# Key and query evacuation in pairs with pinned transposes, high parts of weights on GpSimd, modulation rows moved into attention

## The chip, the cores and the metric

The kernel runs on one core of one Trainium2 chip. The metric is the time of one execution in microseconds (us), lower is better. It is taken as the median of several executions; one more execution was recorded by the hardware profiler, and every row below is from that one. Engines are called TensorE (PE in the rows; PEld is its weight load), VectorE (DVE), ScalarE (ACT), GpSimd (POOL) and SyncE (SP, which issues the DMAs).

## The reference, cut to what matters

The model has two layers over 512 latent tokens of width 1024. Layer 0 mixes by attention (12 query heads, 4 key heads, 64 wide, over 512 latent and 256 context keys) and by a Fourier transform of four groups; layer 1 is a convolution module. Each layer ends with a squared-ReLU MLP, and every sub-layer is scaled and shifted by rows computed from the conditioning vector. What the change touches is this part of layer 0:

```python
def project(h):
    p = h @ w_in
    q = rms_norm(p[..., :D_Q].reshape(bsz, l, N_Q_HEADS, HEAD_DIM), q_g)
    k = rms_norm(p[..., D_Q:D_Q + D_KV].reshape(bsz, l, N_KV_HEADS, HEAD_DIM), k_g)
    v = p[..., D_Q + D_KV:D_Q + 2 * D_KV].reshape(bsz, l, N_KV_HEADS, HEAD_DIM)
    f = p[..., D_Q + 2 * D_KV:]
    return q, k, v, f
...
qx = apply_rope(qx, cos, sin)
kx = apply_rope(kx, cos, sin)
```

The rows of modulation are `m = s @ ada_w + ada_b` with `s = silu(c)`, 6 x 1024 values per layer.

## The kernel before

Products keep the accuracy of 32-bit floats by splitting each operand into a high and a low part in a rounded format: every product is three matmuls, high by high, high by low, low by high (`products`, lines 322 to 324; `three`, lines 184 to 186). Weights come in blocks of 1 MB: SyncE loads one into a `raw` tile (two buffers), an engine writes the high part into `w` and another subtracts it from `raw` for the low part. In `Stream.split` the high part is ScalarE's (line 164); who makes the low part (line 167) says the table `EARLY`, 0 for VectorE and 1 for GpSimd: blocks 3, 4, 5 of the input projection, both Fourier blocks and the first output block were GpSimd's. Each projection or Fourier block is split in pieces of 512 or 516 columns.

The order of the program is: load, conditioning and normalization (to about 40 us of the span); keys and values; queries; attention; then the output projection, the MLPs and the convolution. Rows are handled in tiles of 128 tokens. Keys and values have six tiles (`kv`, two of context `chl` and four latent `act`), each with 24 matmuls of 512 columns in two halves with the weight blocks w0 and w1, into the six banks `kv_ps`. The inputs of the second half are made by `context(1)` and `latent(1, h)` through `affine_split`: GpSimd makes an affine row `aff` (line 220), ScalarE the high part, VectorE subtracts (line 221). Queries come in two groups `g` of four tiles: group 1 is four heads and the Fourier columns, group 2 eight heads; each tile has 24 matmuls.

`evac_kv` takes a key tile out of its bank: ScalarE copies the values and squares the keys, VectorE sums (`ss`, line 505) and makes the inverse root in `rsqrt_small` (lines 208 to 213, with a logarithm and an exponential on ScalarE between), scales (`kn`, line 515), applies gain or rotation (`kr`), and the high and low part go into a stage `st` (lines 525 to 528). Eight transposes by TensorE (line 532) and two copies (line 537) put it into `kA` and `kB`. `evac_q` does the same for queries (lines 549 to 559), with `rq` for the inverse root. The transposes' banks `tbank` have two buffers, `st` has two. The 14 evacuations of one tile each stand in the program behind the products of their stage, and a scheduler in the tile layer may move any instruction that is not pinned (`pin`, `tc.keep_in_program_order`).

The modulation rows are VectorE's: one `gemv_tile` (line 231) multiplies a 128x1024 tile of weights `gv` by a broadcast vector and accumulates into `mods`. The program has 80 of them. `gemv(n, pool, per)` loads `per` tiles by one DMA and does them. With `GV = (0, 3)` twelve stand in the evacuation of group 1's query tiles, three behind each, one tile for each DMA into the pool `gvp`, and the scheduler moves them up; with `GV_AT = (8, 10)` two loads of two tiles each follow the groups 8 and 10 of attention's units.

Attention has 48 units (`softmax`): scores (lines 446 and 448), a maximum on VectorE (line 451), the exponential on ScalarE, the division on GpSimd (line 458), a `flip` by transposes (line 634), and `weigh` on the values. Four units are a group; three units (`AHEAD`) are scored ahead of the first flip.

## Time and profile before

| what | value |
|---|---|
| median of 3 runs | 1216.81 us |
| runs, lowest and highest | 1213.05 and 1807.99 us |
| profiled execution | 1216.12 us |
| its span, first to last instruction | 1214.2 us |
| mean granted clock of TensorE | 0.989 of full |
| TensorE busy | 1175.0 us, 97% of the span |
| VectorE, ScalarE, GpSimd busy | 770.3, 510.7, 196.4 us |

The profiled execution lies between the lowest and the median run, and 1.9 us of it are outside the span. Busy shares are means over stages with different limits, so a change in one stage is read from that stage's own rows. Times in the rows are microseconds from the start of the span.

### The profile page before, as it was taken

To read this page: it belongs to the slowest core of one execution; us is meant where nothing else is said; L and a number is where in the kernel's file an instruction comes from. 1 tells how busy PE (TensorE), PEld (TensorE's weight loads), DVE (VectorE), ACT (ScalarE), POOL (GpSimd) and SP (SyncE) were. 2 spreads that over 40 slices of the span, in tenths; PEclk is the share of its full clock that TensorE was granted. 3 is DMA by queue.
4 is the path that set the end of the run, shared out by engine and by line. 5 is a ranking of instruction groups with operands and counts; after the bars stand their busy time and mean duration, and the time that the engine had idled before them with its cause. 6 is when DMAs were issued, how large, how long until landed. Compare 5 with 4: busy or idle time off the path is not lost.

```text
span 1214.2 us, 16309 instructions
## 1 busy us (share of the span) xinstructions
PE 1175.0 (97%) x6356; PEld 983.0 (81%) x6356; DVE 770.3 (63%) x1395; ACT 510.7 (42%) x931; POOL 196.4 (16%) x236
## 2 busy tenths in 40 slices
PE   5988889999999999999999999999999999999998
PEld 2666777667998888888888988889998888888887
DVE  5797767655787665576465889989953343443431
ACT  5545477774443232142232624387641231331320
POOL 3653243430000000000003037640000000000000
PEclk9998999999999999999999999999999999999999
DMA  8652114105356655544543232613332322233201
GB/s 321 255 189 76 53 35 139 36 1 209 104 174 242 213 204 208 204 176 178 205 173 104 72 113 84 226 64 139 106 104 104 104 104 90 84 104 104 101 21 52
DMA packets 26204, 160.22 MB, mean 132 GB/s; under 512 B 2704, under 2 KB 5776, under 8 KB 8464
## 3 DMA queue, kind: packets, MB, share of 16 engines
q1 hardware_dynamic: 26128, 159.19, 36.7%
q8 instruction: 50, 0.82, 0.3%
q14 instruction: 26, 0.21, 0.1%
HBM read 157.08 MB, written 2.10 MB: 131 GB/s over the span
## 4 chain that ended last, share of the span: by engine, by line
PE 88%; DVE 6%; DMA 1%; POOL 1%; issue 1%; ACT 1%; SPq 0%; DVEq 0%; ACTq 0%; POOLq 0%
PE mm L185 24%; PE mm L186 24%; PE mm L184 24%; PE po L651 3%; PE mm L879 3%; PE tp L634 3%; PE sc L446 2%; PE sc L448 1%; POOL aff L220 1%; DVE gv L231 1%; DMA gv<-in_adat 1%; DMA cx<-in_ctxT 1%; PE sc L324 1%; DVE sm L451 0%; PE tp L384 0%
## 5 line engine op out<-in xcount | busy, mean ns | idle before, releaser
L185 PE MATMUL mm<-act,w 128*128 128x512 f32 (+1 forms) x992 | 338.2, 342 | 0.6 <-DVE act L1061 0.5
L186 PE MATMUL mm<-act,w 128*128 128x512 f32 (+1 forms) x992 | 337.5, 341 | 0.0
L184 PE MATMUL mm<-act,w 128*128 128x512 f32 (+1 forms) x992 | 337.3, 342 | 0.0
L164 ACT ACTIVATE w<-raw 128x1024 fp32r<-128x1024 f32 (+2 forms) x204 | 178.7, 909 | 240.5 <-PE mm L186 202.0
L184 PE MATMUL mm<-f,w 128*128 128x512 f32 (+1 forms) x560 | 207.8, 371 | 0.0
L185 PE MATMUL mm<-f,w 128*128 128x512 f32 (+1 forms) x560 | 207.8, 371 | 0.0
L186 PE MATMUL mm<-f,w 128*128 128x512 f32 (+1 forms) x560 | 207.7, 371 | 0.0
L185 PEld LDWEIGHTS mm<-act,w 128*128 128x128 f32 x992 | 187.8, 190 | 22.6 <-DVE act L1061 1.4
L184 PEld LDWEIGHTS mm<-act,w 128*128 128x128 f32 x992 | 187.2, 190 | 22.2 <-ACT act L1071 0.7
L186 PEld LDWEIGHTS mm<-act,w 128*128 128x128 f32 x992 | 187.8, 190 | 21.4
L167 DVE TENSOR_TENSOR w<-raw,w 128x1024 fp32r<-128x1024 f32 (+1 forms) x172 | 179.8, 1074 | 26.4 <-ACT w L164 26.3
L767 DVE SCALAR_TENSOR_TENSOR x<-mm,mods,x 128x512 f32<-128x512 f32 (+1 forms) x82 | 55.8, 684 | 171.6 <-PE mm L186 171.5
L167 POOL TENSOR_TENSOR w<-raw,w 128x512 fp32r<-128x512 f32 (+2 forms) x32 | 57.9, 1829 | 460.2 <-ACT w L164 460.1
L821 DVE TENSOR_TENSOR rsq<-relu 128x512 f32<-128x512 f32 (+1 forms) x76 | 45.8, 607 | 122.7 <-ACT relu L818 122.6
L818 ACT ACTIVATE relu<-mm 128x512 f32<-128x512 f32 (+1 forms) x76 | 40.3, 530 | 195.4 <-PE mm L186 194.3
L185 PEld LDWEIGHTS mm<-f,w 128*128 128x128 f32 x560 | 105.5, 188 | 18.5 <-DVE f L822 0.3
L184 PEld LDWEIGHTS mm<-f,w 128*128 128x128 f32 x560 | 105.5, 188 | 18.2
L186 PEld LDWEIGHTS mm<-f,w 128*128 128x128 f32 x560 | 105.5, 188 | 18.0
L231 DVE SCALAR_TENSOR_TENSOR gv<-gv,sbc 128x1024 f32<-128x1024 f32 x80 | 99.4, 1256 | 9.8 <-DMA gv<-in_adat 9.8
L868 DVE SCALAR_TENSOR_TENSOR sb<-u,vecs,sb 128x512 f32<-128x512 f32 x112 | 75.3, 749 | 0.0
L451 DVE TENSOR_REDUCE sm<-sc 128x1 f32<-128x768 f32 x48 | 45.9, 955 | 25.5 <-PE sc L448 24.2
L458 POOL TENSOR_SCALAR p<-p,sm 128x768 f32<-128x768 f32 x48 | 47.1, 982 | 73.8 <-DVE sm L457 49.8
(232 smaller groups left out, 1377.7 us busy)
## 6 DMA issues: line engine op xcount, KB each, us to landing
raw<-in_w SPq DMA_DIRECT2D x64, 1024.0 KB, 4.8
gv<-in_adat SPq DMA_DIRECT2D x34, 1024.0 KB, 5.3
raw<-in_pw SPq DMA_DIRECT2D x12, 1024.0 KB, 4.9
w<-in_diag SPq DMA_DIRECT2D x8, 1152.0 KB, 5.7
ar<-in_ada SPq DMA_DIRECT2D x8, 1024.0 KB, 9.4
raw<-in_w_in SPq DMA_DIRECT2D x6, 1024.0 KB, 5.5
gv<-in_adat SPq DMA_DIRECT2D x12, 512.0 KB, 4.5
raw<-in_w_out SPq DMA_DIRECT2D x4, 1024.0 KB, 4.9
```

The costliest lines, as they stand in the source:

```text
L164: hi = nc.scalar.activation(w[:, 0, r], raw[:, r], AF.Copy)
L167: eng.tensor_tensor(w[:, 1, r], raw[:, r], w[:, 0, r].bitcast(F32), ALU.subtract)
L184: nc.tensor.matmul(ps, lhsT=whi, rhs=xhi, start=first, stop=False)
L185: nc.tensor.matmul(ps, lhsT=whi, rhs=xlo, start=False, stop=False)
L186: nc.tensor.matmul(ps, lhsT=wlo, rhs=xhi, start=False, stop=last)
L231: nc.vector.scalar_tensor_tensor(r, r, 1.0, sbc, ALU.mult, ALU.mult, accum_out=mod(l, j, t))
L451: nc.vector.tensor_reduce(sm[:, 0:1], sc[:, :NK], AX.X, ALU.max)
L458: nc.gpsimd.tensor_scalar(p, p, sm[:, 3:4], 0.0, ALU.mult, ALU.add)
L767: nc.vector.scalar_tensor_tensor(xs, ps, mod(l, j, t), xs, ALU.mult, ALU.add)
L818: nc.scalar.activation(r, ps, AF.Relu)
L821: nc.vector.tensor_tensor(s, r, r, ALU.mult)
L868: tap = nc.vector.scalar_tensor_tensor(vs if j == TAPS - 2 else a, u[:, t, j:j + S], w[j], a, ALU.mult, ALU.add)
```

## The change

- `HIGH_POOL` names blocks whose high part GpSimd makes now, by a copy with rounding (CAST in the order): the input projection's blocks 2 to 5 and both Fourier blocks. `EARLY` is gone: the low parts of all these blocks are VectorE's; the first output block's low part stays GpSimd's.
- `rsqrt_small` becomes `rsqrt_pair`: one inverse root for two tiles, and the factor that came behind it is folded into scale and addend. Fourteen become seven.
- `evac_kv` becomes `keys(n)` for a pair of key tiles, which ends at the stage `st`, and `place_key`, which does the transposes and copies later. The scaling `kn` is made by ScalarE as four copies of 64 columns with a scale for each head. `evac_q` becomes `queries` and `place_query` in the same way. `st` has four buffers, the root's tiles two.
- The products of this stage and the transposes of the placements, but those of the last two query tiles, are pinned to the order in which they are written. The second half of key tiles 2 to 5 moves behind `keys(0)`, and `QUERY_ORDER` with the list `after` says after which product slot a placement stands.
- `GV` is gone, and `GV_AT` has eight groups: 16 modulation tiles in attention, by eight loads of 1 MB, where there were four.

```diff
+HIGH_POOL = (2, 3, 4, 5, 6, 7)
...
-GV = (0, 3)
-GV_AT = (8, 10)
+GV_AT = (4, 5, 6, 7, 8, 9, 10, 11)
...
-EARLY = (0, 0, 0, 1, 1, 1, 1, 1, 1, 0, 0, 0)
+QUERY_ORDER = ((0, 0), (0, 1), (1, 0), (1, 1), (0, 2), (0, 3), (1, 2), (1, 3))
...
         def split(self, k, eng, w, raw, r):
-            hi = nc.scalar.activation(w[:, 0, r], raw[:, r], AF.Copy)
-            if k in PINNED:
-                tc.keep_in_program_order(hi)
+            if k in HIGH_POOL:
+                self.high(k, eng, w, raw, r)
+            else:
+                hi = nc.scalar.activation(w[:, 0, r], raw[:, r], AF.Copy)
+                if k in PINNED:
+                    tc.keep_in_program_order(hi)
...
-    def rsqrt_small(pool, dst, ss, n, dim, post):
-        v = pool.tile([P, 16], F32, name="rss_v", tag="rss_v")[:, :n]
-        y = pool.tile([P, 16], F32, name="rss_y", tag="rss_y")[:, :n]
-        nc.vector.tensor_scalar(v, ss, 1.0 / dim, EPS, ALU.mult, ALU.add)
+    def rsqrt_pair(pool, dst, ss, n, scale, add):
+        v = pool.tile([P, 16], F32, name="rss_v", tag="rss_v", bufs=2)[:, :2 * n]
+        y = pool.tile([P, 16], F32, name="rss_y", tag="rss_y", bufs=2)[:, :2 * n]
+        nc.vector.tensor_scalar(v, ss, scale, add, ALU.mult, ALU.add)
         nc.scalar.activation(y, v, AF.Ln)
         nc.scalar.activation(y, y, AF.Exp, scale=-0.5)
         nc.vector.tensor_tensor(v, v, y, ALU.mult)
         nc.vector.scalar_tensor_tensor(v, v, -0.5, y, ALU.mult, ALU.mult)
-        nc.vector.scalar_tensor_tensor(dst, v, 1.5, y, ALU.add, ALU.mult)
-        if post != 1.0:
-            nc.vector.tensor_scalar_mul(dst, dst, post)
+        nc.vector.scalar_tensor_tensor(dst, v.rearrange("p (a n) -> p a n", a=2), 1.5,
+                                       y.rearrange("p (a n) -> p a n", a=2), ALU.add, ALU.mult)
...
-    blocks = [(w_in[i], (vec_, pool_)[EARLY[i]], 4) for i in range(6)]
-    blocks += [(dft[i], (vec_, pool_)[EARLY[6 + i]], 2) for i in range(2)]
-    blocks += [(w_out[i], (vec_, pool_)[EARLY[8 + i]], OUT_CUT) for i in range(4)]
+    blocks = [(w_in[i], vec_, 4) for i in range(6)]
+    blocks += [(dft[i], vec_, 2) for i in range(2)]
+    blocks += [(w_out[i], (pool_, vec_)[i > 0], OUT_CUT) for i in range(4)]
...
-        def products(ps, unit, w, half):
+        def products(ps, unit, w, half, fixed=False):
...
+                for a, e, first, last in ((hi, 0, kt == 0, False), (hi, 1, False, False),
+                                          (lo, 0, False, kt == KT - 1)):
+                    i = nc.tensor.matmul(ps, lhsT=a, rhs=w[:, e, k], start=first, stop=last)
+                    if fixed:
+                        pin(i)
...
-                products(kv_ps[n_], kv[n_], w1, 1)
+                products(kv_ps[n_], kv[n_], w1, 1, True)
             for h in range(2):
                 latent(1, h)
-                for n_ in (2 + 2 * h, 3 + 2 * h):
-                    products(kv_ps[n_], kv[n_], w1, 1)
...
-            def evac_kv(ps, kt, tt):
...
-                rsqrt_small(wk, rk, ss, NKV, HD, 1.0)
-                kn = wk.tile([P, 512], F32, name="kn", tag="kn", bufs=2)[:, :256]
-                nc.vector.tensor_tensor(heads(kn, NKV), heads(kp, NKV),
-                                        rk.unsqueeze(2).to_broadcast([P, NKV, HD]), ALU.mult)
...
+            def transposed(st, step, dst, fixed):
+                pt = tbank()
+                for h in range(4):
+                    i = nc.tensor.transpose(out=pt[:, h * P:(h + 1) * P],
+                                            in_=st[:, h * step:h * step + 128], identity=ident)
+                    if fixed:
+                        pin(i)
+                nc.scalar.activation(dst, pt.rearrange("p (h t) -> p h t", h=4), AF.Copy)
+
+            stages = {}
+
+            def keys(n):
+                ss = wk.tile([P, 16], F32, name="ss", tag="ss", bufs=2)[:, :2 * NKV]
+                for i in range(2):
+                    ps = kv_ps[n + i]
+                    sumsq(ps[:, 0:256], NKV, ss[:, i * NKV:(i + 1) * NKV])
+                    nc.scalar.activation(vS[:, kv[n + i][2]], ps[:, 256:512], AF.Copy)
+                rk = wk.tile([P, 2, NKV], F32, name="rk", tag="rk", bufs=2)
+                rsqrt_pair(wk, rk, ss, NKV, 1.0 / HD, EPS)
+                for i in range(2):
+                    _, _, kt, tt = kv[n + i]
+                    kn = wk.tile([P, 512], F32, name="kn", tag="kn", bufs=2)[:, :256]
+                    for h in range(NKV):
+                        r = slice(h * HD, (h + 1) * HD)
+                        nc.scalar.activation(kn[:, r], kv_ps[n + i][:, r], AF.Copy,
+                                             scale=rk[:, i, h:h + 1])
+                    kr = wk.tile([P, 512], F32, name="kr", tag="t2", bufs=2)[:, :256]
+                    if tt is None:
+                        nc.vector.tensor_tensor(heads(kr, NKV), heads(kn, NKV),
+                                                bc_heads(gs[:, 2], NKV), ALU.mult)
+                    else:
+                        rope_apply(kr, kn, tk, tt, NKV)
+                    st = wk.tile([P, 1024], F32, name="st", tag="st", bufs=4)
+                    sk = st[:, :NKV * 192].rearrange("p (h e d) -> p h e d", h=NKV, e=3)
+                    nc.scalar.activation(sk[:, :, 0].bitcast(F32R), heads(kr, NKV), AF.Copy)
+                    nc.vector.tensor_tensor(sk[:, :, 1].bitcast(F32R), heads(kr, NKV), sk[:, :, 0],
+                                            ALU.subtract)
+                    nc.scalar.activation(sk[:, :, 2].bitcast(F32R), heads(kr, NKV), AF.Copy)
+                    stages["k", n + i] = st
+
+            def place_key(n):
+                st = stages.pop(("k", n))
+                kt = kv[n][2]
                 for e, dst in ((0, kA), (1, kB)):
+                    transposed(st[:, e * 64:], 192, dst[:, :, kt * P:(kt + 1) * P], True)
...
-            def evac_q(ps, tt, h0, n):
...
+            def queries(ps, g, t0):
+                n, h0 = ((4, 8), (8, 0))[g - 1]
+                ss = wk.tile([P, 16], F32, name="ss", tag="ss", bufs=2)[:, :2 * n]
+                for i in range(2):
+                    sumsq(ps[t0 + i][:, :n * HD], n, ss[:, i * n:(i + 1) * n])
+                rsqrt_pair(wk, rq[:, t0:t0 + 2, h0:h0 + n], ss, n, 1.0, HD * EPS)
+                for i in range(2):
+                    tt = t0 + i
+                    qr = wk.tile([P, 512], F32, name="kn", tag="kn", bufs=2)[:, :n * HD]
+                    rope_apply(qr, ps[tt][:, :n * HD], tq, tt, n)
+                    st = wk.tile([P, 1024], F32, name="st", tag="st", bufs=4)
+                    sq_ = st[:, :n * 128].rearrange("p (h e d) -> p h e d", h=n, e=2)
+                    nc.scalar.activation(sq_[:, :, 0].bitcast(F32R), heads(qr, n), AF.Copy)
+                    nc.vector.tensor_tensor(sq_[:, :, 1].bitcast(F32R), heads(qr, n), sq_[:, :, 0],
+                                            ALU.subtract)
+                    if g == 1:
+                        evac_f(ps[tt][:, 256:], tt)
+                    stages[g, tt] = st
+
+            def place_query(g, tt, fixed=True):
+                n, h0 = ((4, 8), (8, 0))[g - 1]
+                st = stages.pop((g, tt))
                 for q4 in range(n // 4):
+                    transposed(st[:, q4 * 512:], 128,
+                               qT[:, h0 + q4 * 4:h0 + q4 * 4 + 4, tt * P:(tt + 1) * P], fixed)
 
...
-            for n_, (_, _, kt, tt) in enumerate(kv):
-                evac_kv(kv_ps[n_], kt, tt)
-                if tt is not None:
-                    gemv(GV[0], gvp, 1)
+            keys(0)
+            for n_ in range(2, 6):
+                products(kv_ps[n_], kv[n_], w1, 1, True)
+                if n_ >= 4:
+                    place_key(n_ - 4)
+                if n_ % 2 == 1:
+                    keys(n_ - 1)
+            after = {1: [lambda i=i: place_key(i + 2) for i in range(4)], 2: []}
             for g in (1, 2):
                 ps = [mbank(m) for m in SLOTS[g]]
                 w = [split_k(next_w()) for _ in range(2)]
-                for half, j in [(half, j) for half in range(2) for j in range(4)] if g == 1 else \
-                        [(half, j) for j in range(4) for half in range(2)]:
-                    products(ps[j], (act, j), w[half], half)
-                for j in range(4):
-                    if g == 1:
-                        evac_q(ps[j][:, :256], j, 8, 4)
-                        evac_f(ps[j][:, 256:], j)
-                        gemv(GV[1], gvp, 1)
-                    else:
-                        evac_q(ps[j], j, 0, 8)
+                for slot, (half, j) in enumerate(QUERY_ORDER):
+                    products(ps[j], (act, j), w[half], half, True)
+                    if after[g]:
+                        after[g].pop(0)()
+                    if slot in (3, 7):
+                        queries(ps, g, slot // 2 - 1)
+                        if g == 1 or slot == 3:
+                            after[g if slot == 3 else 2] += [lambda: None] + [
+                                lambda g=g, t=t: place_query(g, t)
+                                for t in (slot // 2 - 1, slot // 2)]
+            for t in (2, 3):
+                place_query(2, t, False)
             for n_ in range(AHEAD):
                 score(n_)
 
```

The order of instructions on TensorE before, around the end of the key products and the first transposes (`sc` and `po` are the banks of products, `tp` those of transposes, `st` the stages of key tiles; `w1_142` is the second weight block, `w2_511` the third):

```order
L323 MATMUL sc_101<-w1_142,act_79 128x512
L324 MATMUL sc_101<-w1_142,act_79 128x512
L532 MATMUL tp_706<-ident_67,st_702 128x128 x4
L532 MATMUL tp_712<-ident_67,st_702 128x128 x4
L322 MATMUL sc_100<-w2_511,act_79 128x512
L323 MATMUL sc_100<-w2_511,act_79 128x512
L324 MATMUL sc_100<-w2_511,act_79 128x512
L532 MATMUL tp_740<-ident_67,st_736 128x128 x4
L532 MATMUL tp_746<-ident_67,st_736 128x128 x4
```

The order on TensorE now, from the key products of the third pair to the third placement:

```order
L326 MATMUL po_103<-w1_142,act_79 128x512 x12
L326 MATMUL sc_101<-w1_142,act_79 128x512 x12
L511 MATMUL tp_755<-ident_67,st_658 128x128 x4
L511 MATMUL tp_761<-ident_67,st_658 128x128 x4
L326 MATMUL sc_101<-w1_142,act_79 128x512 x12
L511 MATMUL tp_779<-ident_67,st_669 128x128 x4
L511 MATMUL tp_785<-ident_67,st_669 128x128 x4
L326 MATMUL sc_100<-w2_511,act_79 128x512 x12
L511 MATMUL tp_871<-ident_67,st_725 128x128 x4
L511 MATMUL tp_877<-ident_67,st_725 128x128 x4
```

The first two placements stood behind all key products with three products between them; now the first stands ahead of the last 12 key products, and each is 12 products behind the one before, up to the sixth.

The order on GpSimd before, at the end of the affine rows (`aff`) from which VectorE makes the low parts of the second half's inputs, and at the first rotation tables (`tq`, `tk`):

```order
L220 TENSOR_SCALAR aff_603<-xx_96,gain_75,mods_73 128x256
L220 TENSOR_SCALAR aff_607<-xx_96,gain_75,mods_73 128x256
L220 TENSOR_SCALAR aff_611<-xx_96,gain_75,mods_73 128x256
L220 TENSOR_SCALAR aff_615<-xx_96,gain_75,mods_73 128x256
L480 TENSOR_TENSOR tq_657<-tabs_653,gs_655 128x64
L481 TENSOR_TENSOR tk_658<-tabs_653,gs_655 128x64
```

The order on GpSimd now at the same place:

```order
L222 TENSOR_SCALAR aff_579<-xx_96,gain_75,mods_73 128x256
L222 TENSOR_SCALAR aff_583<-xx_96,gain_75,mods_73 128x256
L158 CAST w2_511<-raw2_512 128x512 x4
L222 TENSOR_SCALAR aff_587<-xx_96,gain_75,mods_73 128x256
L222 TENSOR_SCALAR aff_591<-xx_96,gain_75,mods_73 128x256
L481 TENSOR_TENSOR tq_606<-tabs_602,gs_604 128x64
```

The four high parts of the third weight block (CAST), which were ScalarE's, stand now between the sixth and the seventh of the last eight affine rows.

The order on VectorE before, at the start of the first key chain (`w2_511` is the low part of the third weight block, `gv1` a modulation tile):

```order
L167 TENSOR_TENSOR w2_511<-raw2_512,w2_511 128x512 x4
L221 TENSOR_TENSOR act_79<-aff_603,act_79 128x256
L221 TENSOR_TENSOR act_79<-aff_607,act_79 128x256
L221 TENSOR_TENSOR act_79<-aff_611,act_79 128x256
L221 TENSOR_TENSOR act_79<-aff_615,act_79 128x256
L231 SCALAR_TENSOR_TENSOR gv1_1050,mods_73<-gv1_1050,sbc_72 128x1024
L505 TENSOR_REDUCE ss_685<-hsq_686 128x4
L208 TENSOR_SCALAR rss_v_690<-ss_685 128x4
```

And the order on VectorE now at the same place:

```order
L170 TENSOR_TENSOR w2_511<-raw2_512,w2_511 128x512 x4
L223 TENSOR_TENSOR act_79<-aff_579,act_79 128x256
L223 TENSOR_TENSOR act_79<-aff_583,act_79 128x256
L223 TENSOR_TENSOR act_79<-aff_587,act_79 128x256
L223 TENSOR_TENSOR act_79<-aff_591,act_79 128x256
L506 TENSOR_REDUCE ss_633<-hsq_634 128x4
L506 TENSOR_REDUCE ss_633<-hsq_638 128x4
L211 TENSOR_SCALAR rss_v_643<-ss_633 128x8
```

The modulation tile ahead of the first sum is gone, and two sums stand ahead of one root on eight columns.

## Rows read from the trace of the kernel before

**Rows 1.** The page: the span, and the chain that ended last.
```profile
span 1214.2 us, 16309 instructions
...
PE 88%; DVE 6%; DMA 1%; POOL 1%; issue 1%; ACT 1%; SPq 0%; DVEq 0%; ACTq 0%; POOLq 0%
```

**Rows 2.** Busy time (count) by stretch: PE, PEld, DVE, ACT, POOL, clock, DMA, GB/s.
```profile
68.20:157.90 89.70, 73.72 (x342) 59.82 (x342) 69.90 (x166) 43.93 (x116) 28.46 (x31) 0.91 0.31 107
...
194.70:204.60 9.90, 9.90 (x64) 6.81 (x62) 8.92 (x22) 7.43 (x15) 4.62 (x4) 1.00 0.62 210
204.60:215.20 10.60, 10.55 (x65) 7.01 (x64) 7.74 (x21) 7.25 (x15) 3.91 (x5) 1.00 0.31 104
...
232.30:242.10 9.80, 9.80 (x66) 6.76 (x65) 5.47 (x16) 7.32 (x15) 3.61 (x5) 1.00 0.00 0
...
282.80:1214.10 931.30, 927.63 (x4994) 805.12 (x4994) 573.75 (x911) 339.75 (x549) 79.27 (x108) 1.00 0.38 135
```

**Rows 3.** What TensorE waited for, 68.2 to 157.9 us: total, times, longest.
```profile
PE tp L532 <- DVE st L526: 6.5, 3, 3.7
PE tp L556 <- DVE st L550: 3.9, 3, 2.5
PE tp L556 <- DVE sm L452: 2.1, 1, 2.1
```

**Rows 4.** TensorE's timeline: start, duration, line, operation, idle before it.
```profile
73.47 0.39 PE L324 MATMUL sc<-w,act 128*128 128x512 f32 x1
73.70 1.03 PE L532 MATMUL tp<-ident,st 128*128 128x128 f32 x8
...
78.56 1.20 PE L532 MATMUL tp<-ident,st 128*128 128x128 f32 x8 [1.85 <-ACT kA L537]
...
80.41 0.63 PE L324 MATMUL sc<-w,act 128*128 128x512 f32 x1
80.84 0.63 PE L322 MATMUL sc<-w,act 128*128 128x512 f32 x1
```

**Rows 5.** VectorE's groups by shape, 53 to 157.9 us: busy, mean ns, idle before.
```profile
L231 DVE SCALAR_TENSOR_TENSOR gv<-gv,sbc 128x1024 f32<-128x1024 f32 x12 | 16.8, 1403 | 1.1 <-DMA gv<-in_adat 1.1
...
L211 DVE TENSOR_TENSOR rss_v<-rss_v,rss_y 128x4 f32<-128x4 f32 x10 | 3.9, 392 | 1.8 <-ACT rss_y L210 1.8
...
L167 DVE TENSOR_TENSOR w<-raw,w 128x512 fp32r<-128x512 f32 x4 | 2.7, 732 | 0.0
```

**Rows 6.** The chain in 68.2 to 157.9 us, its longest piece.
```profile
88.26 6.68 DMA gv<-in_adat
```

**Rows 7.** VectorE's timeline at the first two key chains.
```profile
66.49 1.34 DVE L231 SCALAR_TENSOR_TENSOR gv<-gv,sbc 128x1024 f32<-128x1024 f32 x1
...
67.77 0.41 DVE L505 TENSOR_REDUCE ss<-hsq 128x4 f32<-128x256 f32 x1
...
69.83 0.42 DVE L515 TENSOR_TENSOR kn<-sc,rk 128x256 f32<-128x256 f32 x1
...
71.31 0.54 DVE L526 TENSOR_TENSOR st<-kr,st 128x256 fp32r<-128x256 f32 x1
...
78.11 1.28 DVE L211 TENSOR_TENSOR rss_v<-rss_v,rss_y 128x4 f32<-128x4 f32 x1
```

**Rows 8.** GpSimd's timeline: a table product, a low part, a division in attention.
```profile
68.26 0.32 POOL L480 TENSOR_TENSOR tq<-tabs,gs 128x64 f32<-128x64 f32 x1
...
78.10 1.27 POOL L167 TENSOR_TENSOR w<-raw,w 128x512 fp32r<-128x512 f32 x1 [4.11 <-ACT w L164]
...
175.01 0.91 POOL L458 TENSOR_SCALAR p<-p,sm 128x768 f32<-128x768 f32 x1 [0.66 <-DVE sm L457]
```

**Rows 9.** ScalarE's groups by shape, 53 to 157.9 us.
```profile
L504 ACT ACTIVATE hsq<-sc 128x256 f32<-128x256 f32 x6 | 2.2, 372 | 0.1
...
L209 ACT ACTIVATE rss_y<-rss_v 128x4 f32<-128x4 f32 x10 | 2.0, 204 | 11.5 <-DVE rss_v L208 11.4
```

**Rows 10.** Modulation tiles in 157.9 to 282.8 us: duration min, median, max.
```profile
L231 DVE SCALAR_TENSOR_TENSOR gv<-gv,sbc x6: 1205/1219/1857, 194.9 to 217.7; 128x1024 f32<-128x1024 f32 x6
```

48 lines of the change are left out of this document (removed).

## The prediction

> **What bounds the kernel now.** I read the page first: the span is 1214.2 us, and 88% of the chain that ended last is TensorE [rows 1]. The table by stretch then shows where TensorE is not the limit in practice. From 282.80 us to the end it is busy 927.63 of 931.30 us at full clock [rows 2]; nothing that this change touches can shorten that part, because the order of instructions behind attention is the same. The stretch 68.20 to 157.90, in which keys and queries are evacuated while TensorE multiplies, has TensorE busy for 73.72 of 89.70 us only, at a mean granted clock of 0.91 [rows 2]. It is the one stretch with something to win, so it is the one I cost.
>
> The floor of that stretch is the work TensorE has in it. One 128x512 product follows the next after 0.23 us at full clock (73.47 to 73.70 [rows 4]; 0.227 over longer runs). The code leaves 216 of them for the stretch: 24 of the last two key tiles, which end at 73.70, and 24 for each of eight query tiles. That is 216 x 0.227 = 49.0 us. Twelve groups of eight transposes at 1.03 us each [rows 4] are 12.4 us. The three score units and the first Fourier products that stand before the first flip are some 3.7 us. Sum 65.1 us. The stretch takes 89.70, so **24.6 us** are lost: 16.0 idle (89.70 - 73.72), and 8.6 in which products run at the lower clock: after the wait of 1.85 us at 78.56 they stand 0.43 us apart, 80.41 to 80.84 [rows 4], which is 1.2 GHz in place of 2.4.
>
> Who is waited for? The view of TensorE's waits names VectorE: 6.5 us for the staged keys, 3.9 for the staged queries, 2.1 for a softmax maximum [rows 3]. Following the chain back through that stretch, it runs through VectorE, and VectorE in turn waits for modulation rows: the longest piece is 6.68 us of a modulation transfer [rows 6]. The twelve modulation tiles there take 16.8 us of VectorE [rows 5]. So the stage is a chain of small VectorE work that arrives late, with TensorE's queue behind it.
>
> **The change, part by part.**
>
> *Modulation tiles out of the stage.* VectorE loses 16.8 us of work and the wait for rows with it. They do not vanish: attention now holds 16 tiles in place of four, two per group of four units. One costs 1.22 us (median) there [rows 10]. A quiet group of four units takes 9.80 us with VectorE busy 5.47 [rows 2]; two tiles make it 5.47 + 2.44 = 7.9, below 9.8. The trace has such groups: 9.90 us with VectorE at 8.92, and 10.60 with it at 7.74 [rows 2]. So the price of one group lies between 0 and 0.8 us, for eight groups 0 to 6.4. If VectorE had no room at all it would be twelve extra tiles, 14.6 us. I take +1, nearer to the first row, since TensorE is 100% busy in it with more on VectorE than the new groups hold. On SP's queue the transfers, 8 of 1 MB, stand between weight loads; that share of the DMA engines is small here (0.31 and 0.62 with one or two of them in a group [rows 2]).
>
> *Inverse roots for pairs.* Fourteen chains become seven. A chain on four columns costs VectorE four small instructions; the largest is 392 ns in the mean [rows 5], inflated by cases such as the 1.28 us at 78.11 [rows 7]. With 0.2 to 0.4 us for each, seven chains fewer are 6 to 11 us of VectorE.
>
> *Key scaling on ScalarE.* Six VectorE products become 24 activations of 64 columns. The trace has none of that size; it lies between 204 ns for 4 columns and 372 ns for 256 [rows 9]. Four in a row are 0.8 to 1.5 us in the chain of a key tile in place of one 0.42 us product on VectorE [rows 7]; I take 1.0. ScalarE has room (43.93 busy of 89.70 [rows 2]).
>
> *High parts on GpSimd, low parts on VectorE.* VectorE gains 16 low parts of the input projection and the Fourier matrix at some 0.7 us (732 ns in the mean of four [rows 5]), 11 us, that GpSimd made before. Its work in the stretch goes from 69.90 [rows 2] to about 69.9 - 16.8 - 2.5 (six scalings) - 9 + 11 = 52.6. That is far under the floor of 65.1, so VectorE should stop being the limit of the stage on the whole; only single chains can be late. A high part on GpSimd has no row: 64 columns cost 0.32 us and 768 columns 0.91 [rows 8], so 512 columns are some 0.7. The bound above is the low part that GpSimd makes now from two inputs, 1.27 us [rows 8].
>
> That same row carries a danger. While GpSimd's 1.27 us subtraction runs from 78.10, VectorE's four-column product started at 78.11 takes 1.28 us, against 0.39 in the mean of its ten [rows 5, 7, 8]: the two exclude each other. The page "SBUF — State Buffer" of the Trainium skill (section "SBUF: two separate sides") has the rule: a VectorE operation with two inputs in SBUF and a GpSimd operation that reads SBUF take one shared pair of ports in turns, and the later one fully blocks. The trace agrees. By that rule this part of the change works against itself, since every high part is read by GpSimd while VectorE makes the low part of the piece before. Blocked for all of the 16 high parts made inside the stretch, VectorE would stand at 52.6 + 16 x 0.7 = 63.8 us, still under TensorE's 65.1, so the sum does not turn on it, only the length of single waits does.
>
> *Pinned placements, made later.* Here is what the change adds. TensorE's queue now has fixed places for the 14 groups of placing transposes, with 12 or 24 products between two of them (2.7 to 5.4 us of cover). Behind a transpose that is not ready the whole TensorE queue stands, with products that need nothing from it. Going through the new order with the durations above:
>
> 1. The first key placement. Keys(0) stands on VectorE behind the four low parts of the third weight block and the last low parts of the activations; four high parts of 0.7 us now stand among GpSimd's affine rows that these need. In the trace the chain begins at 67.77, behind a modulation tile that started at 66.49 and is gone now [rows 7]. I put the new beginning at 69.2: 66.5 and most of 4 x 0.7 (66.5 if the high parts are hidden, 71.6 at the dear price of 1.27). One sum and the root took 2.06 (67.77 to 69.83), and there is a second sum of 0.41; the four scalings are 1.0; gain, copy and subtraction took 1.6 (from 70.25, the end of the scaling, to 71.85 [rows 7]). Ready at 74.3. TensorE gets there when 12 of the 24 products that end at 73.70 are left: 73.70 - 12 x 0.227 = 71.0. Wait **3.3 us**, and half clock behind it: nine products at 0.43 in place of 0.23, as after 78.56 [rows 4], **2.0 us**.
> 2. The second placement waits for bank copies that ScalarE has behind eight scalings of keys(2): **0.6**.
> 3. The other key and the first ten query placements have 2.7 to 5.4 us of cover each behind a chain that begins a whole tile earlier: **0**. If that cover fails, each is a case like the first.
> 4. The end of the stage. The Fourier bank waits for the last query pair (1.0 to 2.0, I take **1.4**), and the last placement for a subtraction that stands behind two softmax maxima, as the last one does now for 2.1 us [rows 3]: **2.4** with some lower clock.
>
> Sum of losses 3.3 + 2.0 + 0.6 + 1.4 + 2.4 = 9.7 us. The stretch is then 65.1 + 9.7 = 74.8 in place of 89.7: **-14.9**. With +1.0 in attention the span becomes 1214.2 - 13.9 = 1200.3. The profiled execution took 1216.12, 1.9 more than its span; it lies 0.7 under the median of the three runs, 1216.81. Forecast: 1200.3 + 1.9 = **1202 us**.
>
> **The rivals.**
>
> *All placements covered.* The first wait disappears if GpSimd's high parts fit beside the affine rows, and the tail fits behind the scores. Then the stretch falls to its floor: 1214.2 - 24.6 + 1.0 + 1.9 = 1192.5 us. For it speaks VectorE's 52.6 of 65.1; against it the order of the first key chain, where no cover is in sight.
>
> *The modulation tiles cost attention their time.* Softmax maxima stand behind tiles of 1.22 us on VectorE, and the scores' banks behind those. The row with 10.60 us speaks for it [rows 2], the one with 9.90 against. Price 6.4 us in all, 14.6 as the end: 1207 to 1216.
>
> *Slower: the fixed places become the bound.* If ScalarE's and VectorE's chains run one tile late throughout, every placement is like the first: 3.3 + 2.0 = 5.3 us. Against a loss of 24.6 now, it decides from the fifth such wait on (26.5 us); with seven of them and 6.4 us in attention it is 1214.2 - 24.6 + 37.1 + 6.4 + 1.9 = 1235 us. Six key placements follow each other within 12 products, so a late chain is not caught up between them. Against it: VectorE's load falls by 17 us.
>
> *It doesn't do what it says.* High parts at the two-input price, 1.27, make the first wait 4 x (1.27 - 0.7) = 2.3 us longer, and VectorE, blocked for longer, may be late by 1 us at four or five more places: 1208 to 1209.
>
> **How the numbers follow.** Forecast as written, 1197 to 1206: 0.60. All covered, about 1192: 0.13. Modulation in attention or the dear high parts, 1207 to 1216: 0.22. Slower than before: 0.05. The range that leaves 2 in 10 out reaches to most of the covered case below and to the middle of the dear cases above: 1193 to 1212. A measurement of this kernel tells some 2% from no change, which is below 1192.5 or above 1241. Below: 0.09, most of the covered case's lower half and a tail. Above: 0.02. Between: 0.89.
>
> **What would show it.** The first flip of attention should begin near 143 us in place of 157.9; TensorE's idle time between 68 and that point should be some 7 us, its largest piece about 3.3 us before the first key placement, waiting for the staged tile. Groups of four units in attention should stay under 10 us with two modulation tiles each. The stretch behind attention should last 931 us as now. I am wrong if the longest waits stand at query placements in the middle of the stage, if high parts on GpSimd take over 1 us, or if attention's groups grow to 10.6 us.

## The result and the profile after

The changed kernel takes **1202.86 us** (median of 4 runs, 1202.18 to 1203.32) against 1216.35 us for the kernel before in the same comparison: ratio 0.9898, 95% interval 0.9877 to 0.9919. The forecast was 1202 us, with a range of 1193 to 1212. The profiled execution took 1203.32 us with a span of 1201.5. One of the four runs of the kernel before took 1807.99 us; the median holds it, the ratio leaves it out.

The page of the changed kernel, the span and the chain that ended last (before: [rows 1]):

```profile
span 1201.5 us, 16248 instructions
...
PE 90%; DVE 4%; POOL 2%; ACT 2%; DMA 1%; issue 1%; SPq 0%; DVEq 0%; ACTq 0%; POOLq 0%
```

The table by stretch of the changed kernel (busy time and count of PE, PEld, DVE, ACT, POOL, then clock, DMA share, GB/s; before: [rows 2]). The first row is the key and query stage up to the first flip, the next five are groups of four units in attention, the last is everything behind attention:

```profile
68.10:142.00 73.90, 67.47 (x342) 55.64 (x341) 50.90 (x121) 38.34 (x108) 17.52 (x32) 0.98 0.15 52
...
177.90:187.70 9.80, 9.80 (x64) 6.81 (x62) 8.82 (x22) 7.43 (x15) 4.62 (x4) 1.00 0.62 211
187.70:198.80 11.10, 10.88 (x68) 7.08 (x68) 8.87 (x22) 7.07 (x15) 5.24 (x4) 1.00 0.28 98
198.80:210.00 11.20, 10.28 (x66) 6.75 (x66) 9.56 (x23) 7.56 (x16) 6.26 (x4) 1.00 0.57 189
210.00:221.60 11.60, 11.31 (x67) 7.14 (x68) 9.21 (x22) 7.23 (x16) 5.32 (x4) 1.00 0.34 101
221.60:232.10 10.50, 9.65 (x65) 6.38 (x64) 8.89 (x22) 7.21 (x15) 5.32 (x4) 1.00 0.52 190
...
270.30:1201.50 931.20, 927.38 (x4994) 805.55 (x4994) 573.33 (x911) 339.87 (x549) 79.27 (x108) 1.00 0.38 135
```

The stage fell from 89.70 to 73.9 us, with VectorE at 50.90 us in place of 69.90 and the mean clock at 0.98 in place of 0.91. The first flip stands at 142.05 us, where it stood at 157.90: 15.85 us gained. Behind attention nothing moved (931.20 against 931.30). But attention gave 3.3 us back: from the first to the last flip it took 124.92 us (142.05 to 266.98) against 121.61 before (157.90 to 279.51). Each of the five groups in the table starts three modulation tiles, not two (15 starts from 178.00 to 229.80 us); the first took 9.80 us, as a quiet group did before, the other four 10.5 to 11.6. 15.85 - 3.3 = 12.5, and the span is 12.7 shorter.

What TensorE waited for in the stage of the changed kernel (total, times, longest; before: [rows 3]):

```profile
PE tp L511 <- DVE sm L454: 1.9, 1, 1.9
PE tp L511 <- ACT kA L515: 1.8, 1, 1.8
PE tp L511 <- DVE st L543: 1.2, 1, 1.2
PE po L187 <- DVE rss_v L211: 0.7, 1, 0.7
PE po L187 <- ACT ghl L633: 0.6, 1, 0.6
PE tp L511 <- DVE st L567: 0.2, 1, 0.2
```

And TensorE's timeline of the changed kernel at the first three key placements (start, duration, operation, count, idle before it):

```profile
72.20 1.07 PE L511 MATMUL tp<-ident,st 128*128 128x128 f32 x8 [1.25 <-DVE st L543]
73.02 2.99 PE L326 MATMUL sc<-w,act 128*128 128x512 f32 x12
77.83 1.14 PE L511 MATMUL tp<-ident,st 128*128 128x128 f32 x8 [1.82 <-ACT kA L515]
78.73 4.58 PE L326 MATMUL sc<-w,act 128*128 128x512 f32 x12
83.15 1.04 PE L511 MATMUL tp<-ident,st 128*128 128x128 f32 x8
```

The waits view has six waits, 6.4 us together, at the places that the prediction named: the first two key placements and the end of the stage. In between TensorE waits at none of the placements. Behind the first wait twelve products still take 2.99 us, full clock; behind the second 4.58.

### The profile page after: what moved, and what is told of

Its sections match the earlier page's. It is cut to its first block, busy times and chain, and to the rows that moved or that the text cites. A ratio compares the mean times of both kernels' runs of the same rounds, so it can differ in the third digit from the quotient of the medians.

```text
span 1201.5 us, 16248 instructions
## 1 busy us (share of the span) xinstructions
PE 1169.5 (97%) x6356; PEld 978.4 (81%) x6356; DVE 763.6 (64%) x1369; ACT 503.4 (42%) x921; POOL 191.7 (16%) x240
## 4 chain that ended last, share of the span: by engine, by line
PE 90%; DVE 4%; POOL 2%; ACT 2%; DMA 1%; issue 1%; SPq 0%; DVEq 0%; ACTq 0%; POOLq 0%
PE mm L189 24%; PE mm L187 24%; PE mm L188 24%; PE po L676 3%; PE mm L904 3%; PE tp L659 2%; PE sc L326 2%; PE sc L448 2%; PE po L326 1%; PE sc L450 1%; POOL aff L222 1%; PE tp L511 1%; DVE sm L453 1%; POOL p L460 1%; DMA cx<-in_ctxT 1%
## 5 line engine op out<-in xcount | busy, mean ns | idle before, releaser
L167 ACT ACTIVATE w<-raw 128x1024 fp32r<-128x1024 f32 (+1 forms) x184 | 166.9, 940 | 238.7 <-PE mm L189 201.7
L170 DVE TENSOR_TENSOR w<-raw,w 128x1024 fp32r<-128x1024 f32 (+2 forms) x188 | 192.6, 1052 | 29.4 <-ACT w L167 26.2
L170 POOL TENSOR_TENSOR w<-raw,w 128x1024 fp32r<-128x1024 f32 (+1 forms) x16 | 34.9, 2201 | 405.2 <-ACT w L167 405.2
L460 POOL TENSOR_SCALAR p<-p,sm 128x768 f32<-128x768 f32 x48 | 53.7, 1120 | 77.9 <-DVE sm L459 60.1
```

What stands on the lines that cost most here:

```text
L167: hi = nc.scalar.activation(w[:, 0, r], raw[:, r], AF.Copy)
L170: eng.tensor_tensor(w[:, 1, r], raw[:, r], w[:, 0, r].bitcast(F32), ALU.subtract)
L460: nc.gpsimd.tensor_scalar(p, p, sm[:, 3:4], 0.0, ALU.mult, ALU.add)
```

## The experiments

Two theories stood against each other. Mine: the stage was a VectorE chain, and moving the modulation tiles out of it was the larger part of the gain. The rivals: the engines of the weights' parts, the pairs or the pins did it. For attention: VectorE's time, or the exclusion between VectorE and GpSimd. Each run was timed against the kernel before on the same chip; "first flip" is the start of the first flip in the run's trace.

**The changed kernel again**, as the measure for the runs beside it.

> The changed kernel itself, as the measure for the runs beside it on this chip: 1202 to 1204 us, first flip at 142 us, all theories alike.

Measured 1204.13 us, ratio 0.9915 (0.9892 to 0.9939), first flip 144.0. So two takings of one kernel lie 1 to 2 us apart in time and in the stage; a difference of that size below is not told from none.

**Modulation tiles moved alone, on the kernel before.**

```diff
-GV_AT = (8, 10)
+GV_AT = (4, 5, 6, 7, 8, 9, 10, 11)
...
-                        gemv(GV[1], gvp, 1)
```

> The kernel before (1216.4 us) with nothing changed but the modulation tiles: none in the key and query stage, 16 in attention. Theory (the stage was a VectorE chain with those tiles and their loads in it): the first flip comes at 145 to 150 in place of 157.9, attention costs 3 us more, time 1208 to 1212 us. Rival (unpinned transposes and single chains hold the stage): first flip within 3 us of 157.9, time 1216 to 1220 us.

Measured 1210.17 us, ratio 0.9957 (0.9943 to 0.9972), first flip 147.11: the stage gave 10.8 us, as my theory said, and attention took 4.3 us of it back (125.93 us for 121.61). Alone, this part gives the stage most of what the whole change gave it (15.85), but 5 of the 13 us in time.

**Modulation tiles back in the changed kernel.** A stage buffer is given up for their two buffers: with four, 4.94 KB of a partition of SBUF are left, and they need 8.

```diff
-GV_AT = (4, 5, 6, 7, 8, 9, 10, 11)
+GV = (0, 3)
+GV_AT = (8, 10)
...
                     if g == 1:
                         evac_f(ps[tt][:, 256:], tt)
+                        gemv(GV[1], gvp, 1)
...
-                    st = wk.tile([P, 1024], F32, name="st", tag="st", bufs=4)
+                    st = wk.tile([P, 1024], F32, name="st", tag="st", bufs=3)
...
```

> The changed kernel with the modulation tiles where they were: twelve in the evacuation of group 1's query tiles, two loads of two tiles behind attention's groups 8 and 10. For their two buffers of 4 KB a stage buffer is given up (three in place of four). Theory (the tiles were a good part of what held the stage): VectorE, busy 50.9 of 73.9 us, gets 17.8 us back and waits for their loads; the first flip comes 5 to 10 us later than 142.05, attention gets 3.3 us back, 1205 to 1210 us. Rival (engines and pinned places made the gain and the tiles only cost in attention): first flip within 2 us, about 1200 us.

Measured 1208.45 us, ratio 0.9949 (0.9932 to 0.9965), first flip 150.74, so 6.7 us later than in the changed kernel beside it, with attention back at 119.35 us. TensorE's timeline of this run shows what the tiles do to the key chains:

```profile
75.12 1.48 PE L513 MATMUL tp<-ident,st 128*128 128x128 f32 x8 [3.95 <-DVE st L545]
86.92 1.06 PE L513 MATMUL tp<-ident,st 128*128 128x128 f32 x8 [2.73 <-DVE st L545]
97.91 1.06 PE L513 MATMUL tp<-ident,st 128*128 128x128 f32 x8 [3.55 <-DVE st L545]
```

Three key placements wait 10.2 us in all for VectorE's staged tile; this is the mechanism of the slower rival, made by the tiles. The buffer given up has no part in these waits: ahead of none of the six staged key tiles does an engine wait for a stage to come free.

**Engines of the weights' parts as before**, high parts on ScalarE, low parts of five blocks on GpSimd.

```diff
-HIGH_POOL = (2, 3, 4, 5, 6, 7)
+HIGH_POOL = ()
...
-    blocks = [(w_in[i], vec_, 4) for i in range(6)]
+    blocks = [(w_in[i], (vec_, pool_)[EARLY[i]], 4) for i in range(6)]
...
```

> The changed kernel with the engines of the weights' parts as before: high parts by ScalarE, low parts of blocks 3 to 5, of both Fourier blocks and of the first output block by GpSimd. Theory (GpSimd's low parts at 1.27 us shut VectorE out longer than its high parts at 0.78 us, and ScalarE's 12 us of high parts stand in the key chains): first flip 2 to 4 us later, 1205 to 1207 us. Rival (the exclusion makes high parts on GpSimd a loss, and VectorE gains 11 us of low parts for nothing): first flip 1 to 2 us earlier, about 1201 us.

Measured 1211.52 us, ratio 0.9969 (0.9959 to 0.9979), first flip 149.53. Dearer than I said by far. GpSimd's, VectorE's and ScalarE's timelines of this run at the third pair of key tiles, and the wait on TensorE that followed:

```profile
82.36 3.75 POOL L171 TENSOR_TENSOR w<-raw,w 128x512 fp32r<-128x512 f32 x3 [3.70 <-ACT w L168]
```

```profile
83.70 1.20 DVE L216 SCALAR_TENSOR_TENSOR rss_v<-rss_v,rss_y 128x8 f32<-128x8 f32 x1
84.94 1.18 DVE L217 SCALAR_TENSOR_TENSOR rk<-rss_v,rss_y 128x8 f32<-128x8 f32 x1
```

```profile
86.16 1.74 ACT L533 ACTIVATE kn<-sc,rk 128x64 f32<-128x64 f32 x8 [2.15 <-DVE rk L217]
87.75 0.65 ACT L516 ACTIVATE kB<-tp 128x512 fp32r<-128x512 f32 x1
```

```profile
88.45 0.75 PE L512 MATMUL tp<-ident,st 128*128 128x128 f32 x4 [3.73 <-ACT kB L516]
```

Two instructions on eight columns take 1.2 us each while GpSimd makes low parts; the scalings and with them ScalarE's queue come late, and TensorE stands for 3.73 us.

This kernel and the one with the modulation tiles moved alone (1210.17 us in the same comparison, first flip 147.11) differ in the pairs, the placements made later and pinned, and ScalarE's scaling; the weights' parts have the same engines in both. The time is no better. So these parts together gain nothing as long as GpSimd makes the low parts. What the low parts on VectorE give without them, and what the pairs give alone, was not tried.

**High parts on ScalarE, low parts on VectorE.**

```diff
-HIGH_POOL = (2, 3, 4, 5, 6, 7)
+HIGH_POOL = ()
```

> The changed kernel with all high parts back on ScalarE, but low parts on VectorE as in the change: half of the run with all engines back (1211.5 us). Theory (ScalarE's queue is what hurt there: its 0.6 us high parts stood ahead of the bank copies, the wait of 3.7 us for kB): most of the loss comes back, first flip 145 to 148 us, 1206 to 1209 us. Rival (GpSimd's low parts, 1.27 us each and shutting VectorE out, were the loss): first flip at 141 to 143 us, 1202 to 1204 us.

Measured 1200.95 us, ratio 0.9880 (0.9861 to 0.9900), first flip 141.13. The rival holds (the time is even below its 1202 to 1204) and my theory on ScalarE falls: the whole loss of the run before was GpSimd's low parts, 1211.52 - 1200.95 = 10.6 us, and the high parts on GpSimd are no gain.

**One block's high parts back on ScalarE.**

```diff
-HIGH_POOL = (2, 3, 4, 5, 6, 7)
+HIGH_POOL = (3, 4, 5, 6, 7)
```

> The changed kernel with one block's high parts back on ScalarE, the third (w_in 2), whose four copies stand among GpSimd's last affine rows. Theory (those 3.2 us delay the first key chain): the first placement comes 2 us earlier, as in the run with all engines back (70.26 in place of 72.20), and 1 to 2 us of it reach the end: about 1201.5 us. Rival (the second placement's bank copies behind the scalings bind anyway): the wait moves to the second placement, no change in time.

Measured 1201.39 us, ratio 0.9890 (0.9871 to 0.9909), first flip 139.97: as the theory said. Against the changed kernel in the same comparison (1204.13 us) it is 2.7 us, and the runs of the two do not overlap (1200.02 to 1201.86, 1203.55 to 1205.17). TensorE's timeline of this run: it has no wait at the first placement, at 70.34; at the second it waits 1.19, at the third 0.56.

```profile
70.34 1.03 PE L511 MATMUL tp<-ident,st 128*128 128x128 f32 x8
71.13 2.98 PE L326 MATMUL sc<-w,act 128*128 128x512 f32 x12
75.31 1.14 PE L511 MATMUL tp<-ident,st 128*128 128x128 f32 x8 [1.19 <-ACT kA L515]
...
79.75 1.14 PE L511 MATMUL tp<-ident,st 128*128 128x128 f32 x8 [0.56 <-ACT kA L515]
```

**No pins.** In the two functions that pin products and transposes:

```diff
-                    if fixed:
-                        pin(i)
```

> The changed kernel with no pin on products and placing transposes; everything else as it is. Theory (the pins keep 12 to 24 products between placements, which covers the chains): the scheduler puts transposes closer to their stages, some waits and lower clock come back, 1204 to 1208 us. Rival (a fixed place is a cost, and the two waits of 1.2 and 1.8 us at the first placements are its price): 1199 to 1201 us.

Measured 1206.54 us, ratio 0.9925 (0.9910 to 0.9940), first flip 142.51. The interval overlaps that of the changed kernel in both of its takings; the stage in the trace is the same to 0.5 us. The theory's transposes closer to their stages do not appear: without pins, too, the key placements and the first four query placements stand 12 or 24 products apart, as they are written. The pins are worth between nothing and some 4 us; this stays open.

**The keys' scaling back on VectorE.**

```diff
-                    for h in range(NKV):
-                        r = slice(h * HD, (h + 1) * HD)
-                        nc.scalar.activation(kn[:, r], kv_ps[n + i][:, r], AF.Copy,
-                                             scale=rk[:, i, h:h + 1])
+                    nc.vector.tensor_tensor(heads(kn, NKV), heads(kv_ps[n + i][:, 0:256], NKV),
+                                            rk[:, i].unsqueeze(2).to_broadcast([P, NKV, HD]), ALU.mult)
```

> The changed kernel with the scaling of the keys back on VectorE, one product of 0.42 us for each tile in place of four copies by ScalarE. Theory (the scalings stand in ScalarE's queue ahead of the bank copies, so the second placement waits 1.8 us, and VectorE has room): the wait at the second placement shrinks to under 1 us, first chain 0.5 us shorter, 1201 to 1203 us. Rival (VectorE is the engine to relieve in this stage): first flip 1 to 2 us later, 1205 us.

Measured 1206.93 us, ratio 0.9926 (0.9906 to 0.9946), first flip 143.8. My theory fails in time: the second placement's wait is gone, as I said, but at the third TensorE waits 2.54 us instead (at 82.11 us, for a bank copy that stands on ScalarE behind a late staged tile), with low clock behind it. The rival's first flip, 1.8 us after 142.05, came, but that of the changed kernel taken again was at 144.0 too. Not told from the changed kernel in time.

**Placements one slot later**, on the run with one block's high parts back.

```diff
-                if n_ >= 4:
-                    place_key(n_ - 4)
+                if n_ == 5:
+                    place_key(0)
...
-            after = {1: [lambda i=i: place_key(i + 2) for i in range(4)], 2: []}
+            after = {1: [lambda i=i: place_key(i + 1) for i in range(5)], 2: []}
```

> The changed kernel with the third block's high parts on ScalarE (1201.4 us by itself) and every key placement one product slot later: the first stands behind all key products. Theory (the waits of 1.2 and 0.6 us at the second and third placement are only a matter of the slot): both go, together with some lower clock behind them, 1198.5 to 1200.5 us. Rival (the bank copies and the key chains are late by their own pace, and the wait moves on to a later placement): 1201 to 1202 us.

Measured 1201.60 us, ratio 0.9892 (0.9874 to 0.9910), first flip 140.82. The rival holds in time: at the second placement TensorE waits 0.94 us for one bank copy and 1.24 for the other. It is not ScalarE's pace that makes them late. ScalarE's timeline of this run, at the two copies of the first placement:

```profile
77.05 0.42 ACT L542 ACTIVATE st<-kr 128x256 fp32r<-128x256 f32 x1 [1.40 <-DVE kr L501]
...
77.68 0.58 ACT L515 ACTIVATE kA<-tp 128x512 fp32r<-128x512 f32 x1
78.95 0.42 ACT L542 ACTIVATE st<-kr 128x256 fp32r<-128x256 f32 x1 [0.69 <-DVE kr L501]
...
79.58 0.57 ACT L515 ACTIVATE kB<-tp 128x512 fp32r<-128x512 f32 x1
```

ScalarE stands idle for 1.40 and 0.69 us ahead of them: each copy is behind a staging copy (`st`) in its queue, and that one waits for VectorE's rotated keys (`kr`).

**Modulation tiles with one input in SBUF.** The product with the broadcast vector is left out of attention's 16 tiles; they are summed by a reduction of the same tile.

```diff
+        if k < 16:
+            nc.vector.tensor_reduce(mod(l, j, t), r, AX.X, ALU.add)
+        else:
             nc.vector.scalar_tensor_tensor(r, r, 1.0, sbc, ALU.mult, ALU.mult, accum_out=mod(l, j, t))
```

> The changed kernel in which attention's 16 modulation tiles are summed by a reduction of the same 128x1024 tile, without the product with the broadcast vector: one input in SBUF in place of two, the same transfers and nearly the same VectorE time (0.95 us for 768 columns means about 1.2 for 1024). It leaves that product out, so the rows of modulation differ. Theory (a tile with two inputs shuts out GpSimd's division p, which takes 1.81 us in place of 0.91 beside it): p falls from 1.12 us in the mean to under 1.0, attention gets 2 to 3 of its 3.3 us back, about 1200.5 us. Rival (VectorE's time alone holds the softmax): attention as in the changed kernel, 1203 us.

Measured 1201.36 us, ratio 0.9892 (0.9874 to 0.9910). The reduction takes VectorE 1.21 us, as long as the product. The groups of GpSimd's division in attention, of the changed kernel and of this run (count, busy, mean ns):

```profile
L460 POOL TENSOR_SCALAR p<-p,sm 128x768 f32<-128x768 f32 x47 | 52.8, 1124 | 73.6 <-DVE sm L459 55.9 <-DVE sm L454 11.5 <-DVE mods L237 4.3
```

```profile
L463 POOL TENSOR_SCALAR p<-p,sm 128x768 f32<-128x768 f32 x47 | 44.2, 940 | 80.1 <-DVE sm L462 60.0 <-DVE sm L457 13.4 <-DVE mods L240 3.8
```

The fifth to tenth groups of four units take 62.1 us, against 64.2 in the changed kernel and 59.8 before. So of the 4.4 us that twelve more tiles cost there, 2.1 go with the exclusion of GpSimd. The other 2.3 stay; VectorE's time in front of the maxima is the likely reason, but no run separates it.

**Tiles in halves**, on the run with shifted placements, with a tile of 32 bytes a partition for the second sums.

```diff
+    modh = const.tile([P, KT], F32, name="modh")
...
+            for i, a in enumerate((mod(l, j, t), modh[:, t:t + 1])):
+                c = slice(i * 512, i * 512 + 512)
+                nc.vector.scalar_tensor_tensor(r[:, c], r[:, c], 1.0, sbc[:, c], ALU.mult, ALU.mult,
+                                               accum_out=a)
...
```

> The kernel with the shifted placements, and attention's 16 modulation tiles multiplied in two halves of 512 columns with a sum for each. VectorE's work grows by some 16 x 0.15 us. Theory (GpSimd's division is shut out for the rest of a tile, 1.2 us at most): with halves it waits 0.6 us at most, p falls from 1.13 to about 1.05 us in the mean, attention gets about 1 us of its 2.1 to 3.3 back, against the run with shifted placements -0.5 to -1 us. Rival (more instructions, more meetings): no gain or +0.5 us.

Measured 1206.76 us, ratio 0.9928 (0.9910 to 0.9946): slower than the run it is built on. And yet the fifth to tenth groups took 58.3 us, better than before the change (59.8). Against the run with shifted placements, attention as a whole took 8.3 us less (118.15 for 126.44). The first flip came 2.4 us later (143.17 for 140.82), and most was lost behind attention, where nothing of the work had changed: from the last flip to the end it took 943.7 us in place of 934.9. The groups of products in 900 to 1150 us of this run (count, busy, mean ns):

```profile
L190 PE MATMUL mm<-f,w 128*128 128x512 f32 x181 | 71.6, 396 | 0.0
L188 PE MATMUL mm<-act,w 128*128 128x512 f32 x183 | 71.3, 389 | 0.0
```

Products of the MLP's second matrix (`f`) take 396 ns each, those of the first 389; without the added tile both take 389. So it is not every product of the rest, as I put it ahead of the next run.

**The best version.** All high parts on ScalarE, and halves whose second sums go into columns of the modulation tile that are free then, so that no tile is added.

```diff
-HIGH_POOL = (2, 3, 4, 5, 6, 7)
+HIGH_POOL = ()
...
+            for i, a in enumerate((mod(l, j, t), mod(1, 5, t))):
+                c = slice(i * 512, i * 512 + 512)
+                nc.vector.scalar_tensor_tensor(r[:, c], r[:, c], 1.0, sbc[:, c], ALU.mult, ALU.mult,
+                                               accum_out=a)
...
```

> The changed kernel with all high parts on ScalarE (1201.0 us by itself) and attention's 16 modulation tiles multiplied in halves of 512 columns; the halves' second sums go to columns of the modulation tile that are free then, so that no tile is added to the pool of constants. The run with halves and an added tile of 32 bytes for each partition had the groups of attention at 58.3 us in place of 64.1 (fifth to tenth group), but every 512-column product of the rest at 230.0 ns in place of 226.7. Theory (the added tile moved the tiles behind it, and that made the products slower; halves themselves free GpSimd): products at 226.7 ns again, 5 us less in attention, 1195 to 1198 us. Rival (the halves' sums or transfers slow the rest): products at 230 ns, 1204 to 1206 us.

Measured **1195.60 us**, ratio 0.9843 (0.9828 to 0.9858), faster than both kernels. The table by stretch of the fifth to tenth groups, of the kernel before, of the changed kernel and of this one, each with its own borders at the scores' starts:

```profile
202.03:261.80 59.77, 59.72 (x382) 40.97 (x382) 37.63 (x98) 43.59 (x90) 23.76 (x25) 1.00 0.15 52
```

```profile
185.16:249.34 64.18, 61.55 (x386) 40.34 (x385) 52.74 (x125) 43.93 (x91) 30.31 (x24) 1.00 0.42 142
```

```profile
182.70:241.02 58.32, 58.32 (x383) 40.73 (x383) 55.28 (x150) 43.52 (x89) 27.00 (x24) 1.00 0.40 135
```

VectorE has the most work in the last row, 55.28 of 58.32 us, and TensorE never waits. And the products behind attention are back:

```profile
L187 PE MATMUL mm<-act,w 128*128 128x512 f32 x192 | 74.7, 389 | 0.0
...
L189 PE MATMUL mm<-f,w 128*128 128x512 f32 x176 | 68.5, 389 | 0.0
```

## Why the prediction was right, point by point

*The floor and the sum.* The time, 1202.86 for 1202, came out of a stage of 73.95 us (68.10 to 142.05) where I had 74.8, and of attention at +3.3 where I had +1.0. The stage was better than the sum by 0.9 and attention worse by 2.3, which left 1.3 us in the profiled execution (1203.32), and the median lies 0.5 below that one. That the two errors have opposite signs is luck.

*The modulation tiles in the stage.* Right: alone they give the stage 10.8 us; taken back into the changed kernel they cost it 6.7. But they are not the larger part of the gain, as I held ahead of the runs: in time they are 5.2 us alone (1210.17 against 1215.39) and 4.3 taken back (1208.45 against 1204.13), where GpSimd's low parts taken back are 10.6.

*The modulation tiles in attention.* Mis-sized: the term was 1.0, with 0 to 6.4 as bounds. Attention as a whole gave back 3.3, and its fifth to tenth groups 4.4 (64.18 - 59.77). By my own sign, groups that grow to 10.6 us, this part was wrong. I took it from a group of 9.90 us with VectorE at 8.92 [rows 2] and reasoned that VectorE's load stays below the group's 9.8. The step that failed is that load is not what counts. The load itself was also larger than forecast, 8.8 to 9.6 us with three tiles in a group for 7.9 with two, yet it stayed below 9.8. GpSimd's division, on the way from the exponential to the flip, is shut out while a tile runs. GpSimd's timeline of the changed kernel beside VectorE's:

```profile
199.36 1.21 DVE L233 SCALAR_TENSOR_TENSOR gv<-gv,sbc 128x1024 f32<-128x1024 f32 x1
...
199.61 1.74 POOL L460 TENSOR_SCALAR p<-p,sm 128x768 f32<-128x768 f32 x1 [0.92 <-DVE sm L459]
```

1.74 us in place of 0.91 [rows 8]. I had this exclusion in the prediction, from 78.10 us of the trace before, and applied it to the key stage only. The run with one input shows that 2.1 us of the 4.4 go with this. The Trainium skill's page "SBUF — State Buffer" (section "Who interferes with whom") says both things that these runs show: a VectorE operation with two inputs in SBUF contends with GpSimd's reads, and a reduction never does. The traces agree, with 1124 ns against 940 for the mean division. Why 2.3 us remain with reductions is open. Halves remove all 4.4 and 1.4 more, although VectorE's work grew. They do not end the exclusion: the division takes 1126 ns in the mean of the fifth to tenth groups, for 1266 in the changed kernel; but beside a half it takes some 1.3 us, where it took 1.74 to 1.81 beside a whole tile, and TensorE no longer waits for it. That points to the length of one instruction. The halves also stand at other places between the maxima, and that was not separated.

*Engines of the weights' parts.* The sum charged 11 us of low parts to VectorE and left open what GpSimd's low parts cost; the runs put their move at 10.6 us, more than any other part. My reading that they were a matter of VectorE's load only was too small: with GpSimd's low parts VectorE is busy for 47.97 us from 66.00 to the first flip at 149.53, without them for 49.03 us from 66.00 to 141.10: less work and a later end. The high parts on GpSimd took 0.78 us each (16 of them, 776 ns in the mean), close to the 0.7 that I bounded, and they are a loss of 2 to 3 us, most of it the four that stand among the affine rows (1201.39 with these alone back against 1204.13 beside it; 1200.95 with all back, in another comparison). The two edits were one line of my sum; they pull in opposite directions.

*The first placements.* Places right, sizes off. The first key chain began at 67.36, not 69.2: GpSimd's last affine row ended at 66.88 with the 3.20 us of high parts in front of it. GpSimd's timeline of the changed kernel:

```profile
56.45 4.59 POOL L222 TENSOR_SCALAR aff<-xx,gain,mods 128x256 f32<-128x256 f32 x6
60.98 3.20 POOL L158 CAST w<-raw 128x512 fp32r<-128x512 f32 x4
64.17 2.71 POOL L222 TENSOR_SCALAR aff<-xx,gain,mods 128x256 f32<-128x256 f32 x2
```

The rows themselves had become shorter. These eight took 7.30 us, for 8.33 before. The four ahead of them ran beside a modulation tile before (VectorE, 53.65 to 54.87), and where the tiles alone are moved they take 1.0 us less. GpSimd's timelines of the kernel before and of that run:

```profile
53.72 3.96 POOL L220 TENSOR_SCALAR aff<-cx,gain,cmod 128x256 f32<-128x256 f32 x4 [7.52 <-DVE mods L397]
```

```profile
53.06 2.94 POOL L220 TENSOR_SCALAR aff<-cx,gain,cmod 128x256 f32<-128x256 f32 x4 [7.48 <-DVE mods L397]
```

The wait was 1.25 for 3.3. No low clock followed it, so the 2.0 for that was nothing there. I had called it the largest of the stage; the largest is 1.87, at the last placement. The second wait was 1.82 for 0.6, for the reason that I gave, the scalings ahead of the bank copy on ScalarE:

```profile
75.55 1.74 ACT L532 ACTIVATE kn<-po,rk 128x64 f32<-128x64 f32 x8 [0.64 <-DVE rk L216]
77.13 0.65 ACT L515 ACTIVATE kA<-tp 128x512 fp32r<-128x512 f32 x1
```

Twelve products behind that wait took 4.58 us in place of 2.99, 1.6 us at the lower clock. 3.3 + 2.0 + 0.6 = 5.9 was forecast for both, 1.25 + 1.82 + 1.6 = 4.7 came.

*The covered placements.* Right: TensorE waits at none of the ten placements between the first two and the last two in the trace of the changed kernel. *The end of the stage.* Right: 0.72 + 0.57 for 1.4, and 1.87 + 0.16 for 2.4.

*The rivals.* The slower one, placements that wait one after the other, does not occur in the changed kernel but does when the tiles come back, three waits and 10.2 us. The dear tiles in attention had 0.22 together with dear high parts; half of that mechanism is what happened.

## What to carry to other kernels

When two engines exclude each other, count every meeting of long and short instructions on the path, not the busy shares: eight-column instructions held for 1.2 us cost more here than 11 us of added VectorE work, and a division of 0.9 us that takes 1.7 was part of attention's loss. Work that fills gaps on a busy engine is worth trying in shorter pieces: halves of the modulation tiles turned a loss of 4.4 us into a gain of 1.4. A change of several parts is worth taking apart even when it wins: one of its parts was a loss of 2 to 3 us.

## What was not expected

A tile of 32 bytes a partition, added to the pool of constants, made the MLP's second products slower, 396 ns for 389 each and 8.8 us in all (943.7 against 934.9 behind attention); the same work without that tile runs as before (934.6). The likely reason is that it moved the tiles behind it in SBUF; which address matters was not tried.

Attention differs by up to 2.7 us between runs with the same work in it, with the clock in its first groups: in the run with shifted placements TensorE's granted clock was 0.91 in 140.8 to 157.8 us, in the run with all high parts on ScalarE 0.99 at the same place, and their attention took 126.4 and 123.8 us. So the whole time of a profiled execution says little on the stage; its first flip does.

```profile
140.80:157.80 17.00, 17.00 (x114) 13.84 (x113) 11.22 (x28) 14.31 (x32) 6.66 (x7) 0.91 0.14 55
```

```profile
141.10:158.10 17.00, 17.00 (x124) 13.90 (x123) 12.13 (x30) 15.19 (x33) 6.66 (x7) 0.99 0.14 56
```
